# A fifth step by seven in four FFN blocks, and seven such steps with five reused sums in the down product's second half

## The chip, the cores and the metric

The kernel runs on one core of one Trainium2 chip. The metric is device time in microseconds (us): the median of three runs before is 1697.33 us (1697.29 to 1697.82). One further execution was profiled. Five engines work in order, each on its own list of instructions, and wait for each other by semaphores: TensorE (PE, matrix products; PEld are its loads of the stationary operand), VectorE (DVE), ScalarE (ACT), GpSimd (POOL, hardly used here) and SyncE (SP, which issues the loads from memory).

## The reference

One layer of a hybrid decoder block over 256 positions of 2048 channels: a projection, attention and a gated recurrence, a merge, an output product, and a feed-forward part (FFN). Only the FFN is touched:

```python
a = rmsnorm(h, norm_ffn_pre[layer])                          # 256 x 2048
gt, up = jnp.split(a @ w_ffn_gate_up[layer], [D_FF], axis=-1)  # D_FF = 5632
ff = (jax.nn.silu(gt) * up) @ w_ffn_down[layer]              # 256 x 2048
h = h + rmsnorm(ff, norm_ffn_post[layer])
```

All is float32. The kernel keeps that accuracy by writing every operand as a high part (rounded to the matrix engine's fast float32 form) and a low part (the rest), and by making each product of three matmuls: high x high, high x low, low x high.

## The kernel before

**Blocks and steps.** A wide block (class `Wide`) makes 1024 output columns for all 256 positions, in eight PSUM banks. The FFN's gate/up product has eleven blocks, j = 0 to 10: 512 columns of the gate and the 512 of up beside them, with 8 steps each. The down product has two blocks ("halves", j = 0 and 1) of 1024 columns, with 22 steps each. A step takes 256 rows of the weights (two tiles of 128, times two groups of 512 columns) and the activations that belong to them (two tiles, times two sides of 128 positions): a 2 x 2 times 2 x 2 product of tiles.

**Full steps and steps by seven.** A full step makes the eight tile products, 24 matmuls of 128 x 512. A step "by seven" makes the same result from seven products of sums, 21 matmuls, in `multiply_wide`: four of the products take sums of weight tiles and three take the weight tiles themselves, called `d` (`dh` and `dl` are their high and low parts; `hi`, named `w` in the profile, and `lo`, named `wl`, are those of a whole tile or of its sums). `by_sums` makes the products with the sums and `by_raw` those with `d`. A step by seven starts with the sums, except the last of its block and those of the down product, which start with `d`. `gather` puts the seven together once a block, behind the last such step.

**The order table.** A block's `order` lists its steps as (m, kind): m is the number of the 256 rows; kind 0 is a full step, 1 a step by seven whose weight sums are made on the spot, 2 a step by seven whose weight sums were made earlier and are fetched (`fetch_sums`, tile `s`). A block takes its steps as they are listed.

**Preparing a step.** `split_wide` prepares a step's weights from its loaded tile `raw`. Kind 0: one ACT copy (L418) and one DVE subtraction (L420) of 2048 columns. Kind 2: two ACT copies (L426) and two subtractions (L427) of 1024, then `dh` (ACT, L429) and `dl` (DVE, L430) of 1536. Kind 1: three sums on DVE (L434, L440, L441), two ACT copies of them (L439, L442), `dh` (ACT, L445), two subtractions (L447) and `dl` (L449). `prepare(i)`, called ahead of step i, splits step i + 2, fetches the ready-made sums of step i + 4 and queues the load of the step whose `raw` buffer comes free; so DVE's and ACT's lists hold these splits in the order of the steps, between a block's evacuation (`gather`, `evac_ffn`, `turn_act`, `evac_down`).

**Buffers.** `raw`, `w` and `wl` have three each, `sum` one, and tag "d", for `dh` and `dl` together, four: those of two steps by seven. Sixteen buffers of 1024 columns (`rslot`) hold, among others, the transposed activations hT (eight in the FFN), the fetched sums `s`, the activations in the down product, and sums of activations (`so`).

**Sums of activations.** `pair_sums` makes them once for hT (`h7`, for m = 0 to 3). In the down product `prep_act` splits the fetched activations (`x.high` on ACT, `x.low` on DVE, L578) and, in a step by seven, makes their sums with `seven_sums` (L522 to L529), kept in `a7[m]`; both halves make their own.

Of the kernel before, what the change touches and what calls it, by code (L numbers as in the profile page):

```python
# [15 lines left out]
F32R = mybir.dt.float32r  # L16
# [8 lines left out]
FF = 5632  # L25
KF = FF // P
# [16 lines left out]
]  # L43
GATE_UP3 = [(3, 0), (4, 0), (0, 2), (5, 0), (1, 1), (6, 0), (2, 2), (7, 0)]
GATE_UP4 = [(4, 0), (5, 0), (0, 2), (6, 0), (1, 1), (2, 2), (3, 1), (7, 0)]
PLACE = (0, 2, 1, 3)
DOWN = [[(m, m in by7) for m in range(KF // 2)] for by7 in (range(4, 20, 3), range(3, 19, 3))]

N_F, N_RAW, N_SPLIT, AHEAD, WARM, BRIDGE = 15, 3, 3, 2, 8, 6

# [50 lines left out]
def tile_hybrid_block(ctx: ExitStack, tc: tile.TileContext, t, out):  # L101
# [13 lines left out]
    def nm(s):  # L115
        serial[0] += 1
        return f"{s}_{serial[0]}"

    def rslot(s):
        return rpool.tile([P, 1024], F32R, tag="r", bufs=16, name=nm(s))  # L120
# [10 lines left out]
    def p3(s, dtype, n, bufs, tag=None):  # L131
        return wide_pool[-1].tile([P, n], dtype, tag=tag or s, bufs=bufs, name=nm(s))
# [72 lines left out]
    def ptile(s):  # L205
        pool, n = (wide_pool[-1], 2) if wide_pool else (fp[0], 5)
        return pool.tile([P, 512], F32, tag="p", bufs=n, name=nm(s))
# [37 lines left out]
    def add_wide_block(*args, **kw):  # L245
        b = Wide(*args, **kw)
        wides.append(b)
        for i in range(len(b.order)):
            n = len(steps)
            slots.append(lambda n=n: load_wide(n))  # L250
            items.append((steps, n, len(slots) - 1))
            steps.append([b, i, None, None])
# [21 lines left out]
    def load_wide(n, pieces=None):  # L274
        b, i = steps[n][:2]
        m, by7 = b.order[i]
        if steps[n][2] is None:
            steps[n][2] = raw_slot()
        if by7 == 2:
            pieces = ((0, (1,)), (1, (0, 1)))  # L280
        raw = steps[n][2]
        for g, ks in pieces or ((0, (0, 1)), (1, (0, 1))):
            at = g * 1024 + ks[0] * 512
            src = b.w[
                (2 * m + ks[0]) * P : (2 * m + ks[-1] + 1) * P, b.cols[g] : b.cols[g] + 512
            ]
            nc.sync.dma_start(
                raw[:, at : at + 512 * len(ks)].rearrange("p (k c) -> p k c", k=len(ks)),
                src.rearrange("(k p) c -> p k c", p=P),
            )  # L290
# [161 lines left out]
    def multiply_wide(n, sides=(0, 1), groups=(0, 1), between=lambda: None):  # L452
# [33 lines left out]
        t, d, sums = w[:2], w[2:], b.seven(m)  # L486
        at = PLACE if by7 == 2 else range(4)
        last = i == b.last7
# [28 lines left out]
    def seven_sums(f, dst):  # L517

        s = ptile("s").rearrange("p (n t) -> p n t", n=4)
        a11, a12, a21, a22 = f[:, 0, :P], f[:, 1, :P], f[:, 0, P:], f[:, 1, P:]  # L520
        for o, x, c, y in ((0, a21, -1.0, a22), (1, s[:, 0, :], -1.0, a11)):
            nc.vector.scalar_tensor_tensor(  # L522
                out=s[:, o, :], in0=x, scalar=c, in1=y, op0=OP.mult, op1=OP.subtract
            )
        nc.vector.tensor_sub(s[:, 2, :], a11, a21)
        nc.vector.tensor_sub(s[:, 3, :], a12, s[:, 1, :])
        return (
            lambda: nc.scalar.activation(dst[:, 0], s, AF.Copy),
            lambda: nc.vector.tensor_sub(dst[:, 1], s, dst[:, 0].bitcast(F32)),  # L529
        )  # L530

    def sums_of(dst):
        return lambda n: (dst[:, 0, n, :], dst[:, 1, n, :])
# [3 lines left out]
    def pair_sums(src, out, slot, pairs=H7):  # L537

        for m in pairs:
            f = ptile("f").rearrange("p (k t) -> p k t", k=2)  # L540
            x = src.slots[m]
            nc.vector.tensor_add(f, x[:, :, 0, :].bitcast(F32), x[:, :, 1, :].bitcast(F32))
            dst = slot().rearrange("p (z n t) -> p z n t", z=2, n=4)
            yield
            for part in seven_sums(f, dst):
                yield
                part()
            out[m] = sums_of(dst)
            yield


    class Split:
# [20 lines left out]
        def high(self, n, src):  # L573
            nc.scalar.activation(self.slots[n][:, :, 0, :], src, AF.Copy)
# [72 lines left out]
    evacs, turns, lanes, queue = deque(), deque(), [deque(), deque()], deque()  # L647
# [507 lines left out]
    h_t, hT = {}, []  # L1155
# [23 lines left out]
    def mix_gain(j, i, b):  # L1179
        if j not in zg:  # L1180
            zg[j] = p3("zg", F32, 1024, 4, "so").rearrange("p (b c) -> p b c", b=2)
        nc.vector.tensor_mul(
            zg[j][:, i, :], b.rest[i, j % 2],
            gpost[j // 2][:, (j % 2) * 512 : (j % 2 + 1) * 512],
        )
# [25 lines left out]
    def residual_of(m, sides=(0, 1), spread=True):  # L1211

        residual(m // 2, m % 2 * 256, m % 2 * 256 + 256, sides, spread)
# [24 lines left out]
    def mix_to_ffn(i):  # L1238
# [60 lines left out]
        ffn(2, 1)  # L1299
        residual_of(5, (0, 1), False)  # L1300

    def more_h(c):
        if c + 1 < KD // 2:
            transpose_in(h_t, colg[:, 16:32], hT[0], c + 1)
        if c == 3:
            mix_gain(3, 1, wides[last_mix])
            residual_of(6, (0, 1), False)
            residual_of(7, (0, 1), False)
            lanes[0].append(second_norm())
        if c == 4:  # L1310
            lanes[1].append(pair_sums(hT[0], h7, lambda: rslot("so"), range(4)))

    def second_norm():
        ss, s2 = small("ss"), small("s2")
# [22 lines left out]
    act_t, h7 = [], {}  # L1337
# [19 lines left out]
    def fetch_act(upto):  # L1357
        while len(act_in) <= min(upto, 2 * len(act_t) - 1, KF // 2 - 1):
            x = rslot("act").bitcast(F32)
            nc.sync.dma_start(x, act_t[len(act_in) % (KF // 4)])  # L1360
            act_in.append(x.rearrange("p (k t) -> p k t", k=4))
# [27 lines left out]
    fss, fz, fpost, parts_of, a7 = [], {}, [], {}, {}  # L1389
# [11 lines left out]
    def prep_act(m, by7):  # L1401

        q = prepared[0] // 2
        prepared[0] += 1
        fetch_act(q + (m % 2 and 2))
        f = act_in[q][:, m % 2 * 2 : m % 2 * 2 + 2, :]
        x = parts_of[m] = Split("a", 2)
        x.high(0, f)
        yield
        x.low(0, f)  # L1410
        if by7:
            dst = rslot("so").rearrange("p (z n t) -> p z n t", z=2, n=4)
            high, low = seven_sums(f, dst)
            high()
            a7[m] = sums_of(dst)
            yield
            low()
# [152 lines left out]
    w = t["w_ffn_gate_up"][0]  # L1570
# [1 line left out]
    add_wide_block(w, (0, FF), PLAIN, lambda k: hT[0](k), None, evac_first, True, mid=more_h)  # L1572
    spare = wides[-1], 0
    for j in range(1, 11):
        add_wide_block(w, (512 * j, FF + 512 * j), GATE_UP4 if j > 1 else GATE_UP3, lambda k: hT[0](k),
                       lambda m: h7[m], evac_ffn, j % 2 == 0,
                       pre=begin_wides if j == 1 else None, turn=1)
    for j in range(2):
        add_wide_block(t["w_ffn_down"][0], (1024 * j, 1024 * j + 512), DOWN[j], act,
                       lambda m: a7[m], evac_down, j % 2 == 0, prep=prep_act,  # L1580
# [120 lines left out]
```

## Time and profile before

| | |
|---|---|
| median of the runs | 1697.33 us |
| the profiled execution | 1698.13 us, span 1696.3 us |
| granted PE clock, mean | 0.998 |
| busy: PE, DVE, ACT | 99%, 85%, 54% of the span |
| DMA | 413.48 MB, mean 244 GB/s |
| a gate/up block of the order `GATE_UP4` | 41.69 to 41.70 us |
| in one such block: DVE busy, ACT busy | 36.47 us, 24.14 us |
| PE idle for another engine, whole run | 1.8 us, all of it before 1006 us |

How to read the rows that follow: times are microseconds from the span's start. A row of the timeline gives start, duration, engine, line, operation, output<-inputs, shape, and in brackets the idle time ahead of it and what ended it. A row of the chain of waits gives start, duration, and what ran (x48: 48 matmuls in a row). A row of stretches gives for each engine its busy time and, in brackets, its instructions, then the granted clock, the share of DMA time and GB/s. A row of waits reads: who waited <- for whom: us in total, times, longest.

### The profile page before, as it was taken

The page shows a single profiled execution, that of the slowest core. Times are in us where ns is not written, and L with a number is a line of the kernel's source. Part 1 is how long each engine was busy: PE and PEld are TensorE (multiplying, and loading weights), DVE is VectorE, ACT ScalarE, POOL GpSimd, SP SyncE. Part 2 cuts the span into 40 slices and gives each one's busy share as a digit, 9 for nine tenths or more (in the row PEclk, how much of TensorE's full clock was granted, in tenths as well). Part 3 has the DMA queues.
Part 4 walks back from the last instruction along what each step waited for, and adds up shares of the span by engine and source line. Part 5 has one row for each costly group of instructions (what it writes and reads, how often), then busy time and mean ns, then how long its engine had stood idle before and what let it go on. Part 6 is the DMA issues. An engine that isn't in the chain of part 4 may idle for free.

```text
span 1696.3 us, 21711 instructions
## 1 busy us (share of the span) xinstructions
PE 1685.2 (99%) x8260; PEld 1416.7 (84%) x8260; DVE 1436.2 (85%) x1662; ACT 914.7 (54%) x1034; POOL 3.9 (0%) x13
## 2 busy tenths in 40 slices
PE   9999999999999999999999999999999999999997
PEld 7888888888888888888888888888888888888886
DVE  6999888867998988885668888888888888898997
ACT  6655555544444434445445547555555555565663
POOL 0000000000000000000000000000000000000000
PEclk9999999999999999999999999999999999999999
DMA  8667666768677767787858646777777777777773
GB/s 285 205 224 243 230 233 228 234 222 309 225 254 252 256 223 243 253 310 275 295 172 275 210 162 227 269 250 252 254 255 253 249 248 272 257 266 256 248 244 130
DMA packets 228904, 413.48 MB, mean 244 GB/s; under 512 B 12816, under 2 KB 79552, under 8 KB 226240
## 3 DMA queue, kind: packets, MB, share of 16 engines
q1 hardware_dynamic: 218544, 373.93, 65.4%
q10 hardware_dynamic: 10192, 38.15, 6.0%
q8 instruction: 64, 1.05, 0.3%
q14 instruction: 40, 0.33, 0.1%
q0 software_dynamic: 64, 0.02, 0.0%
HBM read 376.92 MB, written 35.13 MB: 243 GB/s over the span
## 4 chain that ended last, share of the span: by engine, by line
PE 98%; DVE 1%; ACT 0%; issue 0%; DVEq 0%; ACTq 0%
PE acc L138 62%; PE aux L138 34%; PE aux L930 0%; DVE wl L420 0%; PE aux L610 0%; PE aux L1348 0%; DVE fz L1475 0%; PE acc L1348 0%; ACT w L418 0%; ACT junk L1429 0%; PE aux L597 0%; DVE e L1425 0%; PE aux L1110 0%; DVE yT L578 0%; PE aux L1220 0%
## 5 line engine op out<-in xcount | busy, mean ns | idle before, releaser
L138 PE MATMUL acc<-xT,w 128*128 128x256 f32 (+1 forms) x2048 | 366.8, 338 | 0.0
L420 DVE TENSOR_TENSOR wl<-raw,w 128x2048 fp32r<-128x2048 f32 (+1 forms) x141 | 306.6, 2182 | 68.8 <-ACT w L418 67.1
L138 PEld LDWEIGHTS acc<-xT,w 128*128 128x128 f32 x2048 | 311.9, 188 | 44.7 <-DVE w L365 0.3
L418 ACT ACTIVATE w<-raw 128x2048 fp32r<-128x2048 f32 (+1 forms) x141 | 256.3, 1827 | 109.3 <-PE acc L138 35.1
L364 ACT ACTIVATE w<-raw 128x1024 fp32r<-128x1024 f32 x176 | 185.7, 1058 | 220.5 <-PE acc L138 169.6
L365 DVE TENSOR_TENSOR w<-raw,w 128x1024 fp32r<-128x1024 f32 x176 | 214.8, 1221 | 95.9 <-ACT w L364 95.2
L138 PE MATMUL acc<-w,xT 128*128 128x512 f32 x578 | 169.1, 392 | 0.0
L439 ACT ACTIVATE w<-sum 128x1024 fp32r<-128x1024 f32 x56 | 59.5, 1063 | 177.8 <-DVE sum L434 170.6
L138 PE MATMUL acc<-w,hT 128*128 128x512 f32 x472 | 152.7, 391 | 0.4 <-DVE hT L1232 0.4
L447 DVE TENSOR_TENSOR wl<-sum,w 128x1024 fp32r<-128x1024 f32 x112 | 134.8, 1221 | 13.2 <-ACT w L439 13.2
L138 PEld LDWEIGHTS acc<-w,xT 128*128 128x128 f32 x578 | 108.1, 188 | 22.2
L138 PE MATMUL aux<-w,hT 128*128 128x512 f32 x374 | 120.0, 389 | 0.0
L449 DVE TENSOR_TENSOR dl<-raw,dh 128x1536 fp32r<-128x1536 f32 x56 | 98.3, 1756 | 14.3 <-ACT dh L445 12.2
L138 PE MATMUL aux<-w,xT 128*128 128x512 f32 x344 | 109.8, 389 | 0.0
L138 PEld LDWEIGHTS acc<-w,hT 128*128 128x128 f32 x472 | 88.5, 188 | 19.0 <-DVE hT L1232 0.8
L138 PE MATMUL acc<-wl,hT 128*128 128x512 f32 x236 | 91.9, 389 | 0.0
L445 ACT ACTIVATE dh<-raw 128x1536 fp32r<-128x1536 f32 x56 | 82.7, 1476 | 8.0 <-PE aux L138 4.4
L138 PE MATMUL acc<-w,a 128*128 128x512 f32 x268 | 83.7, 389 | 0.0
L138 PE MATMUL aux<-w,a 128*128 128x512 f32 x268 | 83.7, 389 | 0.0
L138 PEld LDWEIGHTS aux<-w,hT 128*128 128x128 f32 x374 | 70.2, 188 | 14.6
L138 PE MATMUL acc<-w,so 128*128 128x512 f32 x234 | 78.8, 391 | 0.0
L138 PEld LDWEIGHTS aux<-w,xT 128*128 128x128 f32 x344 | 64.6, 188 | 13.4
(298 smaller groups left out, 2964.3 us busy)
## 6 DMA issues: line engine op xcount, KB each, us to landing
raw<-in_w_in SPq DMA_DIRECT2D x270, 512.0 KB, 4.8
raw<-in_w_ffn_gate_up SPq DMA_DIRECT2D x156, 512.0 KB, 4.8
raw<-in_w_ffn_down SPq DMA_DIRECT2D x88, 512.0 KB, 5.4
pre<-in_w_ffn_gate_up SPq DMA_DIRECT2D x40, 512.0 KB, 6.5
presum<-pre ACTq DMA_DIRECT2D x20, 1024.0 KB, 4.7
s<-presum SPq DMA_DIRECT2D x40, 512.0 KB, 7.0
raw<-in_w_mix_out SPq DMA_DIRECT2D x32, 512.0 KB, 4.9
act<-acts SPq DMA_DIRECT2D x22, 512.0 KB, 6.5
```

The lines of the kernel that those rows point to most:

```text
L138: nc.tensor.matmul(ps, lhsT, rhs, start=start, stop=stop, skip_group_check=True)
L364: nc.scalar.activation(wh, raw, AF.Copy)
L365: nc.vector.tensor_sub(wl, raw, wh.bitcast(F32))
L418: nc.scalar.activation(hi[:, c], raw[:, c], AF.Copy)
L420: nc.vector.tensor_sub(lo[:, c], raw[:, c], hi[:, c].bitcast(F32))
L439: nc.scalar.activation(hi[:, :1024], s[:, :1024], AF.Copy)
L445: nc.scalar.activation(dhi, d, AF.Copy)
L447: nc.vector.tensor_sub(lo[:, c], s[:, c], hi[:, c].bitcast(F32))
L449: nc.vector.tensor_sub(dlo, d, dhi.bitcast(F32))
```

## The change

Three things. The gate/up blocks j = 3, 5, 7 and 9 take a new order, `GATE_UP5`: five steps by seven in place of four, the fifth on the rows m = 4 with sums on the spot, and all five next to each other. For that, `h7` gets a fifth set of sums; its first four now lie in a pool that the merge stage left (`p3("so")`), the fifth in an `rslot`. In the second half of the down product the steps by seven are m = 2, 4, 7, 10, 13, 16, 18 in place of 3, 6, 9, 12, 15, 18; the sums for 4, 7, 10, 13 and 16 are those of the first half, and only those for 2 and 18 are made anew.

```diff
 GATE_UP4 = [(4, 0), (5, 0), (0, 2), (6, 0), (1, 1), (2, 2), (3, 1), (7, 0)]
+GATE_UP5 = [(5, 0), (6, 0), (0, 2), (2, 2), (1, 1), (3, 1), (4, 1), (7, 0)]
 PLACE = (0, 2, 1, 3)
-DOWN = [[(m, m in by7) for m in range(KF // 2)] for by7 in (range(4, 20, 3), range(3, 19, 3))]
+DOWN = [[(m, m in by7) for m in range(KF // 2)] for by7 in (range(4, 20, 3), (2, 4, 7, 10, 13, 16, 18))]
...
+    def h7_slot():
+        return p3("so", F32R, 1024, 4) if len(h7) < 4 else rslot("so")
+
...
-            lanes[1].append(pair_sums(hT[0], h7, lambda: rslot("so"), range(4)))
+            lanes[1].append(pair_sums(hT[0], h7, h7_slot, range(5)))
...
-        if by7:
+        if by7 and m not in a7:
             dst = rslot("so").rearrange("p (z n t) -> p z n t", z=2, n=4)
...
-        add_wide_block(w, (512 * j, FF + 512 * j), GATE_UP4 if j > 1 else GATE_UP3, lambda k: hT[0](k),
+        order = GATE_UP3 if j == 1 else GATE_UP5 if j in (3, 5, 7, 9) else GATE_UP4
+        add_wide_block(w, (512 * j, FF + 512 * j), order, lambda k: hT[0](k),
                        lambda m: h7[m], evac_ffn, j % 2 == 0,
```

In the changed file the lines behind the first new one are numbered one higher (L450 is L449 of before), and four higher behind `h7_slot`.

How the instructions stand. First DVE, in block j = 3, from the `dl` of its first step by seven with sums on the spot, (1,1), to the `dl` of its last one. Before:

```order
L449 TENSOR_TENSOR dl_9403<-raw_9268,dh_9402 128x1536
L427 TENSOR_TENSOR wl_9437<-s_9348,w_9436 128x1024
L427 TENSOR_TENSOR wl_9437<-s_9349,w_9436 128x1024
L430 TENSOR_TENSOR dl_9443<-raw_9311,dh_9442 128x1536
L434 TENSOR_TENSOR sum_9475<-raw_9352 128x1024
L440 TENSOR_TENSOR sum_9475<-raw_9352,sum_9475 128x512
L441 TENSOR_TENSOR sum_9475<-raw_9352,sum_9475 128x512
L447 TENSOR_TENSOR wl_9474<-sum_9475,w_9473 128x1024 x2
L449 TENSOR_TENSOR dl_9482<-raw_9352,dh_9481 128x1536
```

The same place on DVE with the change, from the `dl` of (1,1) over (3,1) to (4,1):

```order
L450 TENSOR_TENSOR dl_9419<-raw_9282,dh_9418 128x1536
L435 TENSOR_TENSOR sum_9454<-raw_9325 128x1024
L441 TENSOR_TENSOR sum_9454<-raw_9325,sum_9454 128x512
L442 TENSOR_TENSOR sum_9454<-raw_9325,sum_9454 128x512
L448 TENSOR_TENSOR wl_9453<-sum_9454,w_9452 128x1024 x2
L450 TENSOR_TENSOR dl_9461<-raw_9325,dh_9460 128x1536
L435 TENSOR_TENSOR sum_9492<-raw_9368 128x1024
L441 TENSOR_TENSOR sum_9492<-raw_9368,sum_9492 128x512
L442 TENSOR_TENSOR sum_9492<-raw_9368,sum_9492 128x512
L448 TENSOR_TENSOR wl_9491<-sum_9492,w_9490 128x1024 x2
L450 TENSOR_TENSOR dl_9499<-raw_9368,dh_9498 128x1536
```

The fetched-sum step (2,2) has moved ahead of (1,1), and behind the `dl` of (1,1) there now stand two whole preparations with sums on the spot where one of them and one with fetched sums stood.

Second, DVE at the start of the down product's second half, behind the four additions `e` that take the first half out of PSUM. Before (the activations `a` and a plain `wl` of step 2, then step 3, by seven):

```order
L1425 TENSOR_TENSOR e_12659<-acc_11874,e_12659 128x512
L578 TENSOR_TENSOR a_12741<-act_12625,a_12741 128x2x256
L420 TENSOR_TENSOR wl_12744<-raw_12634,w_12743 128x2048
L1434 SCALAR_TENSOR_TENSOR fz_12781<-e_12660,r2c,fpost_11839 128x512
L434 TENSOR_TENSOR sum_12789<-raw_12674 128x1024
```

The same place on DVE with the change, where step 2 goes by seven with new sums of activations (`s`, `so`):

```order
L1429 TENSOR_TENSOR e_12697<-acc_11912,e_12697 128x512
L435 TENSOR_TENSOR sum_12783<-raw_12672 128x1024
L441 TENSOR_TENSOR sum_12783<-raw_12672,sum_12783 128x512
L442 TENSOR_TENSOR sum_12783<-raw_12672,sum_12783 128x512
L579 TENSOR_TENSOR a_12779<-act_12663,a_12779 128x2x256
L523 SCALAR_TENSOR_TENSOR s_12791<-act_12663 128x128
L523 SCALAR_TENSOR_TENSOR s_12791<-s_12791,act_12663 128x128
L526 TENSOR_TENSOR s_12791<-act_12663 128x128
L527 TENSOR_TENSOR s_12791<-act_12663,s_12791 128x128
L448 TENSOR_TENSOR wl_12782<-sum_12783,w_12781 128x1024 x2
L530 TENSOR_TENSOR so_12790<-s_12791,so_12790 128x512
L450 TENSOR_TENSOR dl_12798<-raw_12672,dh_12797 128x1536
```

A plain step (3) further on DVE with the change stands step 4, by seven, with the sums of the first half:

```order
L1438 SCALAR_TENSOR_TENSOR fz_12877<-e_12696,r2c,fpost_11877 128x512
L435 TENSOR_TENSOR sum_12883<-raw_12748 128x1024
L441 TENSOR_TENSOR sum_12883<-raw_12748,sum_12883 128x512
L442 TENSOR_TENSOR sum_12883<-raw_12748,sum_12883 128x512
L579 TENSOR_TENSOR a_12879<-act_12739,a_12879 128x2x256
L448 TENSOR_TENSOR wl_12882<-sum_12883,w_12881 128x1024 x2
L450 TENSOR_TENSOR dl_12891<-raw_12748,dh_12890 128x1536
```

The half's first step by seven stands one step earlier, its second two steps behind it, and the four small operations `s` and the `so` are gone from the second.

## The prediction

> **What bounds the kernel now.** I read the shares and the chain of waits on the page first, then what TensorE (PE) waited for, then the busy time of single blocks.
>
> ```profile
> span 1696.3 us, 21711 instructions
> PE 1685.2 (99%) x8260; PEld 1416.7 (84%) x8260; DVE 1436.2 (85%) x1662; ACT 914.7 (54%) x1034; POOL 3.9 (0%) x13
> PE 98%; DVE 1%; ACT 0%; issue 0%; DVEq 0%; ACTq 0%
> PE aux L138 <- DVE warm L162: 1.2, 1, 1.2
> PE acc L138 <- DVE hT L1232: 0.4, 1, 0.4
> PE acc L138 <- DVE gate L1147: 0.2, 1, 0.2
> ```
>
> The chain that ends last is 98% PE. The last three rows are all that PE waited for in the run, and none lies behind 1006 us, where all edited work runs. So a matmul taken out is time won, as long as no wait takes its place. How near one is stands in two blocks as busy time: the one that works columns 512 of the gate and up weights (j = 1), and a later one.
>
> ```profile
> core 0: us, PE busy (x) PEld busy (x) DVE busy (x) ACT busy (x) POOL busy (x), PEclk, DMA share, GB/s
> 1049.08:1091.46 42.38, 42.38 (x193) 35.18 (x192) 37.82 (x37) 23.52 (x21) 0.00 (x0) 1.00 0.81 271
> 1299.92:1341.62 41.70, 41.70 (x190) 34.62 (x189) 36.47 (x33) 24.14 (x22) 0.00 (x0) 1.00 0.74 254
> ```
>
> In the later block VectorE (DVE) works 36.47 of 41.70 us and idles 5.2. It prepares every step's weights, so it is the engine that could become the bound, and the place to look is where several costly preparations stand in a row.
>
> **What is removed.** A full step is 24 matmuls, a step by seven 21. Four gate/up blocks (j = 3, 5, 7, 9) and the second half of the down product have one more step by seven each: 5 x 3 = 15 matmuls.
>
> ```profile
> 1288.17 10.88 PE aux L138 x48
> ```
>
> The row is from the chain of waits: the two full steps at a block's start take 10.88 us for 48 matmuls, 0.2267 us each. A full step is 5.44 us, a step by seven 21 x 0.2267 = 4.76. The removal is worth 15 x 0.2267 = **-3.40 us**, if nothing else happens. That is 0.20% of the time, and about 0.2% is also what a measurement of this kernel can tell from no change.
>
> **What is added in the four blocks.** A plain step needs one DVE subtraction of 2048 columns; a step by seven with sums on the spot needs three sums, two halves of `wl` and one `dl`. The new order also puts five steps by seven next to each other (2 to 6), the last three with sums on the spot. Before, three stood together, (1,1), (2,2), (3,1), and this is how the last of them ran:
>
> ```profile
> 1260.29 1.05 ACT L442 ACTIVATE w<-sum 128x1024 fp32r<-128x1024 f32 x1
> 1261.24 1.48 ACT L445 ACTIVATE dh<-raw 128x1536 fp32r<-128x1536 f32 x1
> 1262.75 1.76 DVE L449 TENSOR_TENSOR dl<-raw,dh 128x1536 fp32r<-128x1536 f32 x1
> 1264.42 2.35 DVE L427 TENSOR_TENSOR wl<-s,w 128x1024 fp32r<-128x1024 f32 x2
> 1268.36 1.22 DVE L434 TENSOR_TENSOR sum<-raw 128x1024 f32<-128x1024 f32 x1
> 1270.95 2.44 DVE L447 TENSOR_TENSOR wl<-sum,w 128x1024 fp32r<-128x1024 f32 x2
> 1271.06 1.06 ACT L442 ACTIVATE w<-sum 128x1024 fp32r<-128x1024 f32 x1 [0.33 <-DVE sum L441]
> 1273.02 1.49 ACT L445 ACTIVATE dh<-raw 128x1536 fp32r<-128x1536 f32 x1 [0.89 <-PE aux L138]
> 1274.54 1.76 DVE L449 TENSOR_TENSOR dl<-raw,dh 128x1536 fp32r<-128x1536 f32 x1 [1.15 <-ACT dh L445]
> 1277.80 0.39 PE L138 MATMUL acc<-dh,hT 128*128 128x512 f32 x1
> 1278.03 0.39 PE L138 MATMUL acc<-dl,hT 128*128 128x512 f32 x1
> ```
>
> Read the rows from the last upwards. The last step by seven begins with `dh` and `dl`, at 1277.80 and 1278.03. Its `dl` ended at 1274.54 + 1.76 = 1276.30, 1.73 us early. It could not be made sooner: `dh` and `dl` have four buffers, two steps' worth, so `dh` at 1273.02 waited for PE to finish the step by seven two places back (1277.80 - 4.76 = 1273.04). This is the pace of any run of steps by seven: **a step's `dh` starts when the step two before it ends.**
>
> From the same rows come the costs of one preparation with nothing to wait for. From its first sum to its second ScalarE (ACT) copy: 1271.06 - 1268.36 = 2.70. From that copy to the end of `dh`: 1261.24 + 1.48 - 1260.29 = 2.43, so `dh` ends 5.13 after the first sum, `dl` starts at 5.16, DVE is free for its next instruction 1264.42 - 1262.75 = 1.67 later, at 6.83, and `dl` is complete at 6.92.
>
> Now the new block. Let E be the end of its step 2, (0,2). By the rule, `dh` of step 4, (1,1), starts at E and `dl` at E + 1.52 (1274.54 - 1273.02). DVE takes its instructions in order, so behind that `dl` stand the whole preparations of steps 5 and 6:
>
> - `dl` of step 4: from E + 1.52, DVE free at E + 3.19
> - step 5: DVE free at E + 3.19 + 6.83 = E + 10.02
> - step 6: `dh` ends at E + 10.02 + 5.13 = E + 15.15, `dl` at E + 10.02 + 6.92 = E + 16.94
>
> PE has steps 3, 4, 5 to do from E, 3 x 4.76 = 14.28, and then starts step 6 with `dh` and, 0.23 later, `dl`. Without a wait `dl` is read at E + 14.51. It is complete at E + 16.94, and 0.03 pass until another engine sees that (1274.54 against 1273.02 + 1.49): PE waits 0.9 for `dh` and 1.55 for `dl`, **2.46 us in each of the four blocks, +9.84 us**. Steps 4 and 5 are not late: they begin with the sums' products, step 5's `wl` is done at E + 3.19 + 5.03 = E + 8.2 and step 5 starts at E + 9.52. Nor is step 7 behind the wait, a plain one: its `wl`, 2.2 us of DVE behind the last `dl`, is done at E + 19.1, and PE comes to it at E + 21.5. In the stretch between, DVE and no longer PE sets the pace.
>
> Bounds. Is DVE ready for that `dl` at E + 1.52?
>
> ```profile
> 1290.55 2.36 DVE L427 TENSOR_TENSOR wl<-s,w 128x1024 fp32r<-128x1024 f32 x2 [1.15 <-ACT w L426]
> 1294.55 1.28 DVE L1385 TENSOR_TENSOR e<-e,e 128x512 f32<-128x512 f32 x2
> 1295.76 2.28 DVE L420 TENSOR_TENSOR wl<-raw,w 128x2048 fp32r<-128x2048 f32 x1
> ```
>
> Step 2's preparation starts 2.38 us after the block's first matmul (1288.17) and, with the two products behind it, ends at 1295.76. Step 3 now takes 1268.36 - 1264.42 = 3.94, and step 4's sums and `wl` 1273.39 - 1268.36 = 5.03: 1304.73. E is 1299.92 (there step 2 starts, and the second stretch above) + 4.76 = 1304.68. So DVE has nothing to spare: were `dh` not held at all, `dl` would start about 1.5 sooner and the wait would be 0.95 a block (3.8 in all). That is the low end. Upwards, DVE that is full never catches up what it loses to a late copy or a late transfer; I allow 1 us more a block, 3.5 (14 in all), from the wait of 1.15 on ACT in the last fence.
>
> **Transfers.** The same bytes come in another order.
>
> ```profile
> raw<-in_w_ffn_gate_up SPq DMA_DIRECT2D x14, 512.0 KB, 4.6
> s<-presum SPq DMA_DIRECT2D x4, 512.0 KB, 6.7
> SPq L287 <- DVE dl L449: 14.0, 2, 7.2
> ```
>
> A load waits until its `raw` buffer's last reader on DVE is done and lands 4.6 us later; two preparations (3.94 or more each, 7.9 together) stand between it and its use. The two pairs of ready-made sums for steps 2 and 3 are asked for four steps ahead, about 20 us, against 6.7. I cost the new order at nothing; the load queue (SP) then waits on DVE as it does now.
>
> **The down product.** Five sets of sums are not made again, which frees DVE but moves no end: PE did not wait there. What counts is the start of the second half, where two steps by seven (2 and 4) meet the evacuation of the first half.
>
> ```profile
> 1570.19 2.48 DVE L1425 TENSOR_TENSOR e<-acc,e 128x512 f32<-128x512 f32 x4
> 1576.30 1.22 DVE L434 TENSOR_TENSOR sum<-raw 128x1024 f32<-128x1024 f32 x1
> 1579.49 0.28 DVE L522 SCALAR_TENSOR_TENSOR s<-act 128x128 f32<-128x128 f32 x1
> 1580.42 2.35 DVE L447 TENSOR_TENSOR wl<-sum,w 128x1024 fp32r<-128x1024 f32 x2
> 1584.96 0.74 DVE L1434 SCALAR_TENSOR_TENSOR fz<-e,r2c,fpost 128x512 f32<-128x512 f32 x1
> 1585.62 0.68 DVE L578 TENSOR_TENSOR a<-act,a 128x512 fp32r<-128x512 f32 x1
> 1588.43 0.74 DVE L1434 SCALAR_TENSOR_TENSOR fz<-e,r2c,fpost 128x512 f32<-128x512 f32 x1
> 1587.59 0.39 PE L138 MATMUL aux<-dh,a 128*128 128x512 f32 x1
> ```
>
> A step by seven with fresh activation sums holds DVE 1584.96 - 1576.30 = 8.66; without them 1580.42 - 1579.49 = 0.93 and one low part of 0.60 fall away, 7.13; `fz` is 0.66, a plain step 1588.43 - 1585.62 = 2.81. From the end of the four `e` at 1572.65: step 2, `fz`, step 3, `fz`, step 4 = 8.66 + 0.66 + 2.81 + 0.66 + 7.13 = 19.92, and 0.09 to the end of the last `dl`: 1592.66. The half starts at 1587.59 - 3 x 5.44 = 1571.27, and step 4 reads `dl` after 5.44 + 5.44 + 4.76 + 5.44 + 0.23: 1592.58. About 0.1 late; bounds 0 and 0.8 (the same with DVE 4% later), I take **0.1**. Later steps have one step by seven in three and less DVE work than now.
>
> The fifth set of sums of `hT` in block j = 1 costs DVE one addition, four small operations and two halves of a split, about 2.5 us (0.68 + 4 x 0.28 + 0.68, by the rows of 512 and of 128 columns above), in a block where DVE idles 42.38 - 37.82 = 4.56: nothing; if that cover were gone, 2.5. The held sums take five of sixteen buffers in the down product, where hT's eight are free again: nothing.
>
> **Sum**, against the profiled execution's 1698.13 (span 1696.3): -3.40 + 9.84 + 0.1 = **+6.5**, 1704.7. The runs' median, 1697.33, lies 0.8 under the profiled one: **1703.9**.
>
> **The rivals.**
> *Hidden after all (faster).* DVE catches up and only the matmuls show: -3.4, 1693.9. For it: DVE idles 5.2 us a block. Against it: it idles before E, and that time can't be used, since `dh` is held by PE. It decides where the wait falls under 3.40 / 4 = 0.85 a block; two preparations would have to fit in 14.48 - 3.19 = 11.3, 5.6 each in place of 6.83. 5%.
> *Buffers not binding (same).* `dl` of step 4 starts early, 0.95 a block: -3.4 + 3.8 + 0.1, 1697.8. Against it: the 0.89 that ACT waited for PE. 8%.
> *Transfers late too.* 3.5 a block and 0.8 in the down product: -3.4 + 14.8, 1708.7. The block already moves 254 GB/s. 6%.
> *The clock falls in the waits.*
>
> ```profile
> 1686.00:1688.00 2.00, 1.03 (x5) 0.53 (x3) 1.80 (x6) 0.73 (x3) 0.00 (x0) 1.00 0.53 152
> 1688.00:1690.00 2.00, 0.00 (x0) 0.00 (x0) 1.49 (x6) 1.11 (x4) 0.00 (x0) 0.98 0.00 0
> 1690.00:1693.00 3.00, 0.00 (x0) 0.00 (x0) 2.52 (x5) 0.00 (x0) 0.00 (x0) 0.50 0.58 203
> ```
>
> After the last matmul (1687.03) the granted clock stays whole to about 1690 and is then 0.50. A wait of 3 us would halve the clock; 3 us of matmuls at half speed lose 1.5, in four blocks 6: 1709.9. The waits forecast are 0.9 and 1.55 with a matmul between. 3%.
> [...]
>
> **How the numbers follow.** The forecast has 78%, all of it slower by over 0.2%. With the two slower rivals, slower has 87%; same 8%, faster 5%. The range leaves out the hidden case and the clock, and takes in most of the bounds of the wait (1.5 to 3.5 a block): 1700 to 1709.
>
> **What would show it.** Right: in blocks j = 3, 5, 7, 9 PE waits once for ACT `dh` and once for DVE `dl`, about 2.5 us together, right at the start of the last step by seven; those blocks take about 43.5 us and the others 41.7; matmuls fall by 15. Wrong: no such waits and blocks of 41.0, waits at another step (a `w` or a load), or a granted clock under 1.00 in these blocks.

## The result, and the profile after

| | before | with the change |
|---|---|---|
| median of the runs | 1697.32 us (1697.29 to 1697.82) | 1705.89 us (1704.51 to 1707.36, 4 runs) |
| ratio, 95% interval | | 1.0048 [1.0036, 1.0060] |
| the profiled execution | 1698.13 us | 1704.51 us |

The change makes the kernel slower by 8.6 us. The shares on the page of the changed kernel hardly show it:

```profile
span 1702.7 us, 21690 instructions
PE 1683.3 (99%) x8245; PEld 1413.0 (83%) x8245; DVE 1454.8 (85%) x1673; ACT 922.0 (54%) x1041; POOL 3.8 (0%) x13
```

The fifteen matmuls are gone (8260 to 8245) and PE is busy 1.9 us less, but the span is 6.4 us longer. What took their place stands in the view of what PE waited for (whom it waited for, us in total, times, longest):

```profile
PE aux L139 <- DVE dl L450: 5.2, 4, 1.3
PE aux L139 <- ACT dh L446: 3.1, 4, 0.8
PE aux L139 <- DVE warm L163: 1.2, 1, 1.2
```

The first two rows are new, each with four waits. The stretches of blocks j = 3, 4, 1 and 5 show where these are. They are cut at the end of the eight transposes with which PE, two steps into each block, turns the product of the block before:

```profile
core 0: us, PE busy (x) PEld busy (x) DVE busy (x) ACT busy (x) POOL busy (x), PEclk, DMA share, GB/s
1132.15:1175.83 43.68, 41.62 (x186) 33.97 (x186) 40.23 (x37) 24.47 (x22) 0.00 (x0) 1.00 0.66 219
1175.83:1217.52 41.69, 41.69 (x190) 34.61 (x189) 37.13 (x34) 25.61 (x24) 0.00 (x0) 1.00 0.80 276
1048.05:1090.45 42.40, 42.40 (x193) 35.18 (x192) 39.91 (x43) 24.12 (x22) 0.00 (x0) 1.00 0.80 267
1217.52:1261.16 43.64, 41.57 (x187) 33.98 (x186) 40.29 (x37) 24.48 (x22) 0.00 (x0) 1.00 0.67 224
```

A block with five steps by seven (first and last row) takes 43.65 us where 3 x 0.2267 = 0.68 less than 41.69 was to be had, 41.01. So a block loses 2.65 us and wins 0.68. Blocks with four are as before, and the third row is block j = 1, which now makes the fifth sums of hT: DVE works 39.91 us in it where it worked 37.82, and the block takes 42.40 us where it took 42.38. The timeline of block j = 3 (ACT, DVE and PE in turn) shows how the wait comes about:

```profile
1136.73 1.49 ACT L446 ACTIVATE dh<-raw 128x1536 fp32r<-128x1536 f32 x1 [1.05 <-PE acc L139]
1138.25 1.76 DVE L450 TENSOR_TENSOR dl<-raw,dh 128x1536 fp32r<-128x1536 f32 x1 [1.31 <-ACT dh L446]
1139.93 1.22 DVE L435 TENSOR_TENSOR sum<-raw 128x1024 f32<-128x1024 f32 x1
1145.10 1.76 DVE L450 TENSOR_TENSOR dl<-raw,dh 128x1536 fp32r<-128x1536 f32 x1 [0.15 <-ACT dh L446]
1146.78 1.22 DVE L435 TENSOR_TENSOR sum<-raw 128x1024 f32<-128x1024 f32 x1
1150.45 1.47 ACT L446 ACTIVATE dh<-raw 128x1536 fp32r<-128x1536 f32 x1
1151.95 1.76 DVE L450 TENSOR_TENSOR dl<-raw,dh 128x1536 fp32r<-128x1536 f32 x1
...
1150.81 0.39 PE L139 MATMUL acc<-dh,hT 128*128 128x512 f32 x1
1151.97 0.50 PE L139 MATMUL aux<-dh,hT 128*128 128x512 f32 x1 [0.77 <-ACT dh L446]
1153.77 0.50 PE L139 MATMUL aux<-dl,hT 128*128 128x512 f32 x1 [1.29 <-DVE dl L450]
1154.11 0.40 PE L139 MATMUL aux<-dh,hT 128*128 128x512 f32 x1
```

The first `dh` is that of step 4, (1,1): it waits for PE to finish step 2, so E is 1136.7. Its `dl` follows at E + 1.5, and from there DVE does not stop: the sums of step 5 at 1139.93, its `dl`, the sums of step 6 at 1146.78, its `dl` at 1151.95. PE is ready for `dh` of step 6 at 1150.81 + 0.23 = 1151.04 and starts it at 1151.97, 0.93 late. It wants `dl` 0.23 after that, at 1152.20, and gets it at 1153.77, 1.57 late. A last piece is easily missed: the two matmuls behind a wait take 0.50 us, and the next one starts 0.34 us later, not 0.23.

### The profile page after: what moved, and what is told of

Read it like the earlier page. It is cut to its first block, busy times and chain, and to the rows that moved or that the text cites. A ratio compares the mean times of both kernels' runs of the same rounds, so it can differ in the third digit from the quotient of the medians.

```text
span 1702.7 us, 21690 instructions
## 1 busy us (share of the span) xinstructions
PE 1683.3 (99%) x8245; PEld 1413.0 (83%) x8245; DVE 1454.8 (85%) x1673; ACT 922.0 (54%) x1041; POOL 3.8 (0%) x13
## 3 DMA queue, kind: packets, MB, share of 16 engines
q8 instruction: 64, 1.05, 0.3%
## 4 chain that ended last, share of the span: by engine, by line
PE 94%; DVE 3%; ACT 2%; issue 1%; DVEq 0%; ACTq 0%
PE acc L139 61%; PE aux L139 31%; ACT dh L446 1%; DVE sum L435 1%; DVE dl L450 0%; PE aux L931 0%; DVE wl L421 0%; DVE sum L441 0%; DVE sum L442 0%; PE aux L611 0%; PE aux L1352 0%; DVE fz L1479 0%; PE acc L1352 0%; ACT w L419 0%; ACT junk L1433 0%
## 5 line engine op out<-in xcount | busy, mean ns | idle before, releaser
L421 DVE TENSOR_TENSOR wl<-raw,w 128x2048 fp32r<-128x2048 f32 (+1 forms) x136 | 295.4, 2180 | 65.4 <-ACT w L419 63.5
L419 ACT ACTIVATE w<-raw 128x2048 fp32r<-128x2048 f32 (+1 forms) x136 | 246.8, 1823 | 99.0 <-PE acc L139 32.7
L440 ACT ACTIVATE w<-sum 128x1024 fp32r<-128x1024 f32 x61 | 64.8, 1062 | 194.4 <-DVE sum L435 188.5
L448 DVE TENSOR_TENSOR wl<-sum,w 128x1024 fp32r<-128x1024 f32 x122 | 147.2, 1221 | 5.4 <-ACT w L440 5.4
L450 DVE TENSOR_TENSOR dl<-raw,dh 128x1536 fp32r<-128x1536 f32 x61 | 107.2, 1757 | 15.8 <-ACT dh L446 13.0
L139 PE MATMUL aux<-w,hT 128*128 128x512 f32 x318 | 102.8, 389 | 0.0
L446 ACT ACTIVATE dh<-raw 128x1536 fp32r<-128x1536 f32 x61 | 90.0, 1475 | 8.4 <-PE acc L139 4.2
L139 PE MATMUL acc<-w,so 128*128 128x512 f32 x264 | 88.9, 391 | 0.0
L139 PE MATMUL aux<-w,a 128*128 128x512 f32 x254 | 79.5, 389 | 0.0
L139 PE MATMUL acc<-wl,xT 128*128 128x512 f32 x193 | 75.1, 389 | 0.0
```

The source lines that it names most:

```text
L139: nc.tensor.matmul(ps, lhsT, rhs, start=start, stop=stop, skip_group_check=True)
L419: nc.scalar.activation(hi[:, c], raw[:, c], AF.Copy)
L421: nc.vector.tensor_sub(lo[:, c], raw[:, c], hi[:, c].bitcast(F32))
L440: nc.scalar.activation(hi[:, :1024], s[:, :1024], AF.Copy)
L446: nc.scalar.activation(dhi, d, AF.Copy)
L448: nc.vector.tensor_sub(lo[:, c], s[:, c], hi[:, c].bitcast(F32))
```

## The experiments

Three theories were to be told apart first. **A**, that of the prediction: the new order of the four blocks alone costs the time, since the held `d` buffers and then DVE's list make the last step by seven late. **B**: DVE is short of time over the whole of these blocks, in whatever order the steps stand. **C**: the time is lost elsewhere, in the down product or in transfers. Ratios are against the kernel before on the same chip (medians 1698.01 us for the first four, 1697.63 for the next four, 1697.8 for the last two).

### The two halves of the change by themselves

Only the down product changed; gate/up and `h7` as before:

```diff
-            lanes[1].append(pair_sums(hT[0], h7, h7_slot, range(5)))
+            lanes[1].append(pair_sums(hT[0], h7, lambda: rslot("so"), range(4)))
...
-        order = GATE_UP3 if j == 1 else GATE_UP5 if j in (3, 5, 7, 9) else GATE_UP4
+        order = GATE_UP3 if j == 1 else GATE_UP4
```

> Only the down product's part of the change: the gate/up blocks keep the order of before and the four sums of hT. Theory A (the loss is made in the four gate/up blocks alone): three matmuls fewer are worth -0.68 us, and step 4 of the second half waits 0.1 to 0.3 for its dl, so -0.6 to -0.3 us against before. Rival C (the held sums, or the second half's denser start, cost by themselves): slower than before by 1 us or more, with waits of PE behind 1570 us or waits of the load queue for an rslot.

Only the four blocks changed; the down product as before:

```diff
-DOWN = [[(m, m in by7) for m in range(KF // 2)] for by7 in (range(4, 20, 3), (2, 4, 7, 10, 13, 16, 18))]
+DOWN = [[(m, m in by7) for m in range(KF // 2)] for by7 in (range(4, 20, 3), range(3, 19, 3))]
...
-        if by7 and m not in a7:
+        if by7:
```

> Only the gate/up part of the change; the down product is as before. Theory A: four waits for dh and dl at the start of the last step by seven, 2.46 us of PE in each block, and 12 matmuls fewer: -2.72 + 9.84 = +7.1 us by the working of the prediction. Rival C: clearly less than the whole change loses.

Measured: the down product alone 1697.71 us, ratio 0.9998 [0.9989, 1.0007]; the four blocks alone 1706.64 us, 1.0052 [1.0039, 1.0066]. What PE waited for with the four blocks alone:

```profile
PE aux L139 <- DVE dl L450: 5.2, 4, 1.3
PE aux L139 <- ACT dh L446: 3.1, 4, 0.8
```

These are the waits of the whole change, row for row. The loss is all in the four blocks; the down product's half is worth a few tenths that this measurement can't tell from nothing.

### Another order of the same steps

The same five steps by seven, with the two fetched-sum steps between those with sums on the spot:

```diff
-GATE_UP5 = [(5, 0), (6, 0), (0, 2), (2, 2), (1, 1), (3, 1), (4, 1), (7, 0)]
+GATE_UP5 = [(5, 0), (6, 0), (1, 1), (0, 2), (3, 1), (2, 2), (4, 1), (7, 0)]
```

> The whole change, but the five steps by seven of the four blocks stand in the order (1,1), (0,2), (3,1), (2,2), (4,1): the same steps and instructions, and no two preparations with sums on the spot behind each other. Theory A (a wait made by what stands directly behind the held dl): 0 to 0.5 us of waiting in each block, so -3.4 + 0 to 2 + 0.1, that is -3.3 to -1.3 us against before. Rival B (DVE is short over the whole block: 40.2 us of work in 41.0): the wait only moves to another step, 1.5 us or more a block, so +3 us or more against before.

Measured: 1697.11 us, 0.9995 [0.9986, 1.0004]: 0.9 us under before, which this measurement can't tell from nothing, where the change is 8.6 over it; and less of a gain than the 1.3 to 3.3 expected. The timeline of PE in block j = 3:

```profile
1151.80 0.39 PE L139 MATMUL aux<-dh,hT 128*128 128x512 f32 x1
1152.45 0.50 PE L139 MATMUL aux<-dl,hT 128*128 128x512 f32 x1 [0.26 <-DVE dl L450]
1152.79 0.39 PE L139 MATMUL aux<-dh,hT 128*128 128x512 f32 x1
```

`dh` is in time and `dl` of the last step by seven shows a wait of 0.26 us. The block's marks (the first of the eight transposes, in this block and in the next), 1131.88 and 1173.44, are 41.56 apart, 0.55 more than the 41.01 without a wait. Why 0.55 and not 0.26 can be read off these rows: idle time counts from the modelled end of the matmul before (1151.80 + 0.39), 0.16 behind the moment at which the next could have started, and the matmul behind a wait holds the next one back by 0.11. So **a short wait of PE costs what the view of waits shows plus about 0.3 us**: 0.27 by these rows, 0.27 to 0.36 by the lengths of the blocks in all experiments. And the nine microseconds between the two orders come from the same steps with the same work, which speaks against B: here it matters not how many costly preparations a block has, but how many stand in a row.

### Which part is the buffers, which part DVE

Step 2 of the four blocks starts with `d`, so that its `dh` and `dl` come free 12 matmuls (2.72 us) sooner:

```diff
-        first, second = (by_raw, by_sums) if b.prep or last else (by_sums, by_raw)
+        first, second = (by_raw, by_sums) if b.prep or last or (b.order is GATE_UP5 and i == 2) else (by_sums, by_raw)
```

> The whole change in its own order, but step (0,2) of the four blocks makes its products with d first and those with the sums behind them, so that its dh and dl are free 12 matmuls (2.7 us) sooner and the dh of (1,1) needn't wait for the step's end. Theory A: DVE reaches the dl of (1,1) about 1.3 us earlier and the wait falls from 2.46 to about 1.0 to 1.5 us a block: -3.4 + 4 to 6 + 0.1, that is +0.7 to +2.7 us against before. Rival B (DVE short over the whole block, the hold of no importance): as slow as the change itself, +6 us or more.

Measured: 1700.75 us, 1.0016 [1.0007, 1.0025]. The timeline of DVE and PE in block j = 3, whose mark is 1132.19 here and was 1131.11 with the change:

```profile
1138.17 1.76 DVE L450 TENSOR_TENSOR dl<-raw,dh 128x1536 fp32r<-128x1536 f32 x1 [0.15 <-ACT dh L446]
...
1151.88 1.76 DVE L450 TENSOR_TENSOR dl<-raw,dh 128x1536 fp32r<-128x1536 f32 x1
...
1153.69 0.50 PE L139 MATMUL aux<-dl,hT 128*128 128x512 f32 x1 [1.18 <-DVE dl L450]
```

From the block's mark, `dl` of step 4 begins at 5.98 where it began at 7.14, so the hold was worth 1.16 us. DVE's idle time ahead of it falls from 1.31 to 0.15: now DVE's own list is the limit. The wait for `dh` is gone, that for `dl` stays, and the block takes 42.50 (marks 1132.19 and 1174.69). Of the 2.65 us a block, the held buffers are 1.16 and DVE's list is 1.5. Both links of theory A are shown, and the second is the larger.

### The last step by seven starts with its sums

The last step by seven of the four blocks no longer begins with `dh` and `dl`, which PE then wants 12 matmuls later:

```diff
-        first, second = (by_raw, by_sums) if b.prep or last else (by_sums, by_raw)
+        first, second = (by_raw, by_sums) if b.prep or (last and b.order is not GATE_UP5) else (by_sums, by_raw)
```

> The whole change in its own order, but the last step by seven of the four blocks starts with the sums' products, so that dl is read 12 matmuls (2.72 us) later. Theory A: the dl is then in time, and what is late is that step's wl, complete at E + 10.02 + 5.03 = E + 15.05 against E + 14.28: 0.5 to 1.0 us a block in place of 2.65, so -3.4 + 2 to 4 + 0.2, that is -1.2 to +0.8 us against before. Rival D (the gather, which now follows 12 matmuls later, holds up the next block): a new wait at the transposes of the next block, 0.5 us or more.

And this together with the other order above:

> The other order of e3 and the sums-first last step of e7 together. Theory A: the last dl, 0.4 us late in e3, gets 2.7 us more, and no wait is left in the four blocks: all 15 matmuls come through but for 0.2 us in the down product, -3.2 us against before; blocks of 41.0 us. Rival B (DVE short over the whole block: 40.2 us of work in 41.0): waits of 0.5 us a block or more remain somewhere, -1 us or slower.

Measured: alone 1697.65 us, 1.0000 [0.9991, 1.0009]; with the other order **1694.62 us (1693.93 to 1694.84), 0.9983 [0.9974, 0.9992]**, faster than both kernels. Alone, the timeline of PE shows a new wait in the same step, for the low part of the sums:

```profile
1151.58 0.50 PE L139 MATMUL acc<-wl,so 128*128 128x512 f32 x1 [0.42 <-DVE wl L448]
```

0.42 and some 0.3 more is about what the block's three matmuls win, 0.68: the four blocks take 41.73 to 41.79 us where they took 41.69, and the time is that of before. The later gather (rival D) holds nothing up, for the blocks behind them still take 41.69. With both edits, PE's waits in the whole run are

```profile
PE aux L139 <- DVE warm L163: 1.2, 1, 1.2
PE acc L139 <- DVE hT L1233: 0.4, 1, 0.4
PE acc L139 <- DVE gate L1148: 0.2, 1, 0.2
```

and blocks j = 3 and 4 take

```profile
core 0: us, PE busy (x) PEld busy (x) DVE busy (x) ACT busy (x) POOL busy (x), PEclk, DMA share, GB/s
1131.27:1172.29 41.02, 41.02 (x188) 34.08 (x186) 38.45 (x34) 24.13 (x21) 0.00 (x0) 1.00 0.74 258
1172.29:1213.98 41.69, 41.69 (x190) 34.63 (x189) 38.90 (x37) 25.83 (x23) 0.00 (x0) 1.00 0.73 251
```

So the waits are those of the kernel before, and a five-step block takes the 41.01 that the matmuls alone give. The fifteen matmuls are won once the order of the work lets them be.

### More work ahead of the late `dl`, and behind it

One more DVE subtraction of 512 columns in the sums of step 5, (3,1):

```diff
         nc.vector.tensor_sub(s[:, 1536:], raw[:, 1536:], s[:, 1024:1536])
+        if b.order is GATE_UP5 and m == 3:
+            nc.vector.tensor_sub(s[:, 1536:], raw[:, 1536:], s[:, 1024:1536])
```

> The whole change, and in the four blocks the preparation of step (3,1) makes its last sum of 512 columns twice (about 0.7 us of DVE between the held dl and the last one). Theory A: the dl of the last step by seven is later by as much, so each of the four blocks is 0.7 us longer than with the change alone (43.65): 44.35, and the whole 2.8 us slower than the change. Rival C (PE waits there for another thing, such as a transfer): the blocks stay at 43.65.

One more of 512 columns in the split of the block's last step, (7,0), which DVE does behind the late `dl`:

```diff
+            if b.order is GATE_UP5 and m == 7:
+                nc.vector.tensor_sub(lo[:, :512], raw[:, :512], hi[:, :512].bitcast(F32))
```

> The whole change, and in the four blocks the preparation of the full step (7,0) makes 512 columns of its wl twice (about 0.7 us of DVE behind the last dl). Theory A (only what stands ahead of the last dl counts): the four blocks stay at 43.65, the whole as the change. Rival B (DVE short over the whole block): as much as one more sum ahead of it, 0.7 us a block, 2.8 in all.

Measured: ahead of it 1710.94 us (1709.86 to 1715.33), 1.0077 [1.0062, 1.0093]; behind it 1706.34 us (1705.43 to 1706.94), 1.0052 [1.0038, 1.0066], against 1.0048 and, measured again, 1.0051 for the change. DVE's time counts up to the late `dl` and not behind it, as theory A has it. But ahead of it the loss is 4.6 us more than behind it, and theory A asked for 2.8. The four blocks with the work ahead of it, in a profiled execution that was the slowest of its four (1715.33 us):

```profile
core 0: us, PE busy (x) PEld busy (x) DVE busy (x) ACT busy (x) POOL busy (x), PEclk, DMA share, GB/s
1132.28:1176.63 44.35, 41.56 (x187) 33.99 (x186) 41.10 (x38) 24.47 (x21) 0.00 (x0) 1.00 0.63 208
1218.32:1264.31 45.99, 43.20 (x188) 35.13 (x186) 41.59 (x38) 24.47 (x21) 0.00 (x0) 0.96 0.64 212
1306.00:1353.04 47.04, 44.25 (x188) 35.94 (x186) 41.67 (x38) 24.47 (x21) 0.00 (x0) 0.93 0.62 207
1394.74:1441.81 47.07, 44.28 (x187) 35.95 (x186) 41.67 (x38) 24.45 (x21) 0.00 (x0) 0.93 0.62 207
```

The first row is 0.7 us over the change's 43.65, one subtraction of 0.69 us. The other three are 1.6 to 2.7 longer still, at a granted clock of 0.96 and 0.93, and PE is *busy* longer. The kernel with the work behind has one such block of its four (marks 1131.54 and 1176.81, 45.27 us), and this is PE in it:

```profile
1152.40 0.50 PE L139 MATMUL aux<-dh,hT 128*128 128x512 f32 x1 [0.78 <-ACT dh L448]
1154.20 0.59 PE L139 MATMUL aux<-dl,hT 128*128 128x512 f32 x1 [1.29 <-DVE dl L452]
1154.59 0.63 PE L139 MATMUL aux<-dh,hT 128*128 128x512 f32 x1
1155.02 0.63 PE L139 MATMUL aux<-dh,so 128*128 128x512 f32 x1
```

Behind the two waits the matmuls come 0.43 us apart (1154.59, 1155.02) in place of 0.227, for 3.4 us in all: eight matmuls, each 0.2 late, are the 1.6 us. That raised a question for the change itself, whose runs spread over 2.9 us while the kernel with no waits stays within 0.9.

### Does the clock fall in the change too?

The changed kernel once more, and a smaller dose: one more subtraction of 128 columns in the sums of step 5.

```diff
         nc.vector.tensor_sub(s[:, 1536:], raw[:, 1536:], s[:, 1024:1536])
+        if b.order is GATE_UP5 and m == 3:
+            nc.vector.tensor_sub(s[:, 1920:], raw[:, 1920:], s[:, 1408:1536])
```

> The changed kernel itself once more, to see why its runs spread over 3 us and why their median lies above its profiled execution. Clock theory (in some executions the granted clock falls to half for some 3.4 us behind a wait, 15 matmuls at 0.43 us in place of 0.227, 1.6 us or more each): runs from 1704.5 to 1708, and where the profiled span is over 1703.5, one or more of the four blocks is 45.2 or longer in place of 43.65, with a granted clock under 1.00 in the stretch behind the wait. Rival (the spread comes from the loads at the start): all four blocks 43.65, and the first long stretch of matmuls starts later instead.

> One more DVE subtraction of 128 columns in the sums of step 5, (3,1), about 0.25 us. By DVE's list alone the wait for dh grows from 0.77 to about 1.0 in each block: 1.0 us in the run, median 1706.9. Clock theory: the longer wait also makes the clock fall in more of the blocks, between the change (few) and the kernel with a whole extra sum of 512 columns (three of four): median 1707 to 1710, and a profile with one to three blocks of 45.5 to 47. Rival (no such threshold nearby): four blocks of 43.9 and a median within 0.5 of 1706.9.

Measured: the change again 1705.97 us (1705.08 to 1707.72), 1.0051 [1.0038, 1.0063]; the small dose 1709.28 us (1708.18 to 1710.08), 1.0065 [1.0052, 1.0079]. The profiled execution of the former was its fastest, 1705.08, and had no fall (block j = 3: 43.67 us at 1.00), so it neither shows nor excludes a fall in the slower ones. The four blocks with the small dose:

```profile
1132.01:1177.56 45.55, 43.16 (x187) 35.12 (x185) 41.25 (x38) 24.46 (x21) 0.00 (x0) 0.96 0.63 212
1219.25:1263.23 43.98, 41.59 (x187) 33.97 (x186) 40.74 (x38) 24.47 (x21) 0.00 (x0) 1.00 0.64 218
1304.92:1350.49 45.57, 43.18 (x186) 35.14 (x185) 41.18 (x38) 24.46 (x21) 0.00 (x0) 0.96 0.62 213
1392.19:1436.16 43.97, 41.58 (x187) 33.97 (x185) 40.73 (x38) 24.47 (x21) 0.00 (x0) 1.00 0.63 218
```

In two blocks of four the clock fell, each time for a loss of 1.6 us (3.4 us at 0.43 us a matmul is room for eight, not fifteen, and each is 0.2 late); the other two took 43.97, 0.3 more than with the change. The clock theory is shown for the kernels with a longer wait, and in one block for the work behind. Put against each other by PE's idle time in a block as the waits show it:

| kernel | idle, us a block | blocks with a fallen clock |
|---|---|---|
| other order; sums first; early release | 0.26; 0.42; 1.2 | 0 of 12 |
| the change (two profiles); four blocks alone; work behind | 2.06 | 1 of 16 |
| 128 columns more ahead | 2.4 | 2 of 4 |
| 512 columns more ahead | 2.8 | 3 of 4 |

What the falls have in common can be read from their moments. With 512 columns more the clock is down from 1242.81, 1328.14 and 1416.89 us, with 128 columns from 1154.92 and 1329.00. These moments lie 85.33, 88.75 and 174.08 us apart, which is 25, 26 and 51 times 3.413 us, and the falls last 3.41 us, or 6.83 in two of them. So the falls of each of these two executions lie on one grid of steps of 3.413 us, and each lasts one step or two; a stretch between two points of an execution's grid is called a window here. With the work behind, the grid is laid through its one fall, at 1154.46. Cut at these edges, the stretches read, for the work behind, for 512 columns more, and for 128 columns more:

```profile
1151.05:1154.46 3.41, 1.34 (x5) 0.60 (x4) 3.22 (x3) 3.41 (x3) 0.00 (x0) 1.00 0.20 77
1154.46:1157.87 3.41, 3.41 (x9) 2.63 (x9) 3.38 (x3) 1.55 (x2) 0.00 (x0) 0.50 0.76 235
```

```profile
1239.40:1242.81 3.41, 1.77 (x7) 1.24 (x8) 3.22 (x3) 3.41 (x3) 0.00 (x0) 1.00 0.13 11
1242.81:1246.22 3.41, 3.41 (x10) 2.64 (x9) 3.41 (x3) 1.09 (x2) 0.00 (x0) 0.50 0.94 341
```

```profile
1410.92:1414.33 3.41, 1.85 (x7) 0.96 (x6) 3.26 (x3) 3.41 (x3) 0.00 (x0) 1.00 0.50 189
1414.33:1417.75 3.42, 2.59 (x11) 2.17 (x12) 3.38 (x3) 3.03 (x3) 0.00 (x0) 1.00 0.44 127
```

By 3.413 less its busy time, PE idles 2.07, 1.64 and 1.56 us in the first window of each pair; behind the first two the clock is 0.50, behind the third it stays whole. In the four blocks of these three profiles, six windows hold 1.64 to 2.33 us of idle time and a fall follows each of them; the others hold 1.56 or less, and in none of those does the clock begin to fall. So what the six falls share is the idle time in one window, not the length of a wait nor the sum of a block: with 128 columns more, waits of 1.10 and 1.29 us stood at the fall of 1154.92, and waits of 1.09 and 1.30, divided by the edge at 1414.33, left the clock at 1.00. These are six falls in three executions; a limit as such no run shows.

For the table this means that blocks of one execution are no independent trials. A changed and an unchanged block together take 43.65 + 41.69 = 85.34 us, 25 windows, so that all four lie alike to the windows until a fall shifts them by 1.6 us; "1 of 16" is one execution of four. For the change itself it gives an estimate: from 1151.20 to 1153.77 its two gaps idle 2.06 us, and a window holds 1.6 of them (a value between the 1.56 and the 1.64 above) if its edge lies in a certain 1.8 us of every 3.4. If executions lie evenly to the windows, that is about half of them, each losing 1.6 us, 0.8 in the mean. The runs of these blocks do lie in two groups: 1704.5 and 1705.1 against 1706.7 and 1707.4; again, 1705.1 to 1706.0 against 1707.6 and 1707.7; the four blocks alone, 1705.0 to 1706.6 against 1708.0 and 1708.5.

## Why the prediction was right

The forecast was 1703.9 us in a range of 1700 to 1709; the median came out at 1705.89. By its steps:

- **Removed matmuls, -3.40.** Right: 8245 matmuls, a block without a wait takes 41.01, and the kernel with both repairs, which has no wait, is 3.0 us faster than before.
- **The wait, 2.46 a block.** The mechanism and the place were right. `dh` of step 6 was forecast to end at E + 15.15, which is 1151.88 by E of the timeline, and ended at 1150.45 + 1.47 = 1151.92; `dl` at E + 16.94 = 1153.67 and ended at 1151.95 + 1.76 = 1153.71. The size was short by 0.19: the term "0.9 for `dh` and 1.55 for `dl`" put what follows a wait at nothing. Of the 0.19, 0.04 is `dl` itself (read at 1153.77, where 1151.04 + 0.23 = 1151.27 was possible: 2.50), 0.11 is that the matmul behind that wait holds the next back, and the rest lies in the matmuls after it. 2.65 was measured, 0.76 more in four blocks.
- **Rival "buffers not binding", 0.95 a block.** It did not happen, and its price was too low: with the buffers freed early, 1.5 a block stayed. The prediction reckoned that the hold kept `dl` back by 1.5; it was 1.16, since that `dl` began at E + 0.36 (5.98 behind the mark, with E 5.62 behind it) where E + 0.05 was reckoned: 0.16 is DVE's list, 0.15 a wait for ACT's `dh`. Most of the rest is what follows a wait, put at nothing.
- **Transfers, h7, block j = 1: 0.** Right; no load is among PE's waits.
- **Down product, +0.1 against -0.68.** The place was right and the size small. At step 4 of the second half the timeline of the changed kernel reads

```profile
1599.19 0.39 PE L139 MATMUL aux<-dh,a 128*128 128x512 f32 x1
1599.48 0.50 PE L139 MATMUL aux<-dl,a 128*128 128x512 f32 x1
1599.81 0.40 PE L139 MATMUL aux<-dh,a 128*128 128x512 f32 x1
```

  `dl` starts at 1599.48 where 1599.42 was possible, and the next one 0.11 late: 0.17 in place of 0.1.
- **The sum, +6.5 between the two profiled executions.** These differ by 6.38, but that close match is partly luck. The chain's first long stretch of matmuls began at

```profile
8.38 8.21 PE acc L138 x36
```

  in the profile of before and at

```profile
7.33 8.22 PE acc L139 x36
```

  in that of the change, 1.05 sooner, which no edit causes: in five other profiles it lies between 7.20 and 8.47. The ten PE instructions ahead of it, four transposes and six warm-up matmuls, begin at 4.93 in both profiles and take 2.85 us before and 1.80 with the change. Before, the warm-up matmuls start 0.43 us apart up to 7.12 and 0.22 to 0.23 apart from there; with the change they are 0.22 apart from the first, at 5.43. Why, the traces do not show: the stretches read a granted clock of 1.00 there in both. Without these 1.05 us the step is 7.4, which is the corrected sum: -3.40 + 4 x 2.65 + 0.17 = +7.37.
- **From the profile to the median.** The prediction took 0.8 off, as in the kernel before. The medians differ by 8.57, 1.2 more than the corrected sum. The same sum, worked with each kernel's own blocks in which the clock stayed whole, shows where such an excess occurs:

| kernel | sum | measured, medians on one chip | excess |
|---|---|---|---|
| other order | -3.40 + 4 x 0.55 + 0.17 = -1.0 | -0.9 | 0.1 |
| early release | -3.40 + 4 x 1.49 + 0.17 = +2.7 | +2.7 | 0.0 |
| sums first | -3.40 + 4 x 0.75 + 0.17 = -0.2 | 0.0 | 0.2 |
| both repairs | -3.40 + 0.17 = -3.2 | -3.0 | 0.2 |
| four blocks alone | -2.72 + 4 x 2.65 = +7.9 | +8.6 | 0.7 |
| the change, again | +7.4 | +8.2 | 0.8 |
| work behind | +7.4 | +8.7 | 1.3 |
| 128 columns more ahead | -3.40 + 4 x 2.97 + 0.17 = +8.6 | +11.5 | 2.9 |
| 512 columns more ahead | -3.40 + 4 x 3.34 + 0.17 = +10.1 | +13.3 | 3.2 |

  The excess is there only where PE's idle time in a block reaches 2.06 us, and grows with the count of fallen clocks. The measured steps have intervals of 1.5 to 2.6 us either way, so only the last two rows are clear of noise each by itself. So the rival **"the clock falls in the waits"**, given 3% as a case by itself, was a real effect on top of the forecast, and its condition, a wait of 3 us, was too strict: 1.64 us of idle time in one window was enough. Nor does a trace of before show that the clock comes back after 3 us of matmuls, for a loss of 1.5; here it stayed down for 3.41 us or 6.83, for a loss of 1.6 or 2.7. That it makes up the 0.7 to 1.2 us of the change is inferred, from the estimate above and the two groups of runs: none of the change's two profiled executions held a fall, and the slower ones were not profiled.

## What to carry to other kernels

Before putting cheaper steps next to each other, lay their preparations end to end on the engine that makes them, beginning where a buffer is released: an average of 5 us idle in a block did not help, since it did not lie in that run. If the run doesn't fit, change the order or let the late operand be read last; here two edits of one line each turned a loss of 8.6 us into a gain of 3. A wait of PE cost 0.27 to 0.36 us more than the view of waits shows, and in six blocks, where PE's waits put 1.64 to 2.33 us of idle time into one window of 3.413 us, the granted clock fell to 0.50 and took 1.6 or 2.7 us on top.

## What the runs showed of the hardware

- The granted clock fell to half behind two waits of which none was longer than 1.5 us: 0.78 and 1.29 us with one matmul between sufficed once in four executions, 1.10 and 1.29 twice in one, 1.50 and 1.29 three times in one. In the four blocks of the three profiles with falls, a fall followed each of the six windows of 3.413 us that held 1.64 to 2.33 us of idle time, and none that held 1.56 or less. The five falls with 128 and 512 columns more begin whole multiples of 3.413 us apart (25, 26 and 51 of them) within an execution. The clock stayed down for one window in four falls (1.6 us lost each) and for two in the other two (2.7 lost each), where the second wait reached 1.1 us over the window's edge.
- Kernels whose edits all lie behind 1000 us began their first long stretch of matmuls between 7.20 and 8.47 us in seven profiles, so that a difference of two single profiles is uncertain by as much as 1.3 us; the lengths of blocks are not touched by it.
